# Up product of a decoder trunk: two of seven block products without the two leading columns, and the streamed operands at residues 0 and 128 modulo 256 bytes

## The chip, the cores and the metric

The kernel runs on one core of a Trainium2 chip. The metric is the device time of one execution in microseconds. Times are medians of a few executions; the profile is one further execution, whose span and whose own time are both given below. Engines are named as the profile does: PE is TensorE (matmuls; PEld its weight loads), DVE is VectorE, ACT is ScalarE, POOL is GpSimd, SP is SyncE, which issues the DMAs.

## The reference, cut to what matters

One layer of a decoder trunk over 1024 tokens and 16 meta tokens, model width 1024, float32. Two token mixers (a convolution module and a windowed attention) are merged and added to the residual, then comes the feed-forward part, which this change concerns:

```python
h = layer_norm(DEEPNORM_ALPHA * h + mixed @ w_out, ln1_g, ln1_b)
up = causal_dwconv(h @ ffn_w_up, ffn_dw, ffn_dw_b)      # 3 taps, 2 x 2816 channels
u, g = jnp.split(up, 2, axis=-1)
f = (jax.nn.gelu(g, approximate=False) * u) @ ffn_w_down
return layer_norm(DEEPNORM_ALPHA * h + f, ln2_g, ln2_b)
```

The convolution is causal with three taps, so the up product of a token needs that of the two tokens before it. Where the 1024 tokens are cut into two halves of 512, the second half needs the last two columns of the first half's product.

## The kernel before, in words

**Precision.** A float32 product is made of three matmuls in the type float32r: each operand is split into a high and a low part (the high part is a copy by ACT, the low part a subtraction by DVE), and high x high, high x low and low x high are added up in PSUM.

**Stages.** The big input product and the mixers run to about 415 us of the profile, the projections (tile ps_p) to about 512, the rows of the output product with their LayerNorm and their turning into columns (ps_w, ps_h) to about 609, the up product to 1049.6, the down product (ps_x, ps_z at L1619) to the end.

**The up product (L1462 to L1546).** The 1024 input channels are cut into two halves, the 1024 tokens into two halves h = 0, 1, and the output channels into gate and value. This two by two by two product is done by Strassen's scheme in Winograd's form with seven block products instead of eight: B11, B21, BT2, BT4, BT1, BT3, B22, in this order. The names are those of the streamed operand: B11 and the like are blocks of the input h, BT1 to BT4 sums and differences of them, formed once (form_t2, form_t3, form_t4) and split once into high and low parts (bsplit, split_of, L1174 to L1208). The stationary operands, sums of weight blocks, are formed and split anew in each block of output channels (up_weights L1321, wsplit L1299) and looked ahead by nine sets (w_ahead(9) in prod); they go around a ring of ten slots.

The outer loop goes over c = 0 to 21, each with 128 gate channels and 128 value channels. I call one turn of it a block. In a block, prod(q, bank, first) (L1475) does one of the seven products: for each sub, for each of four chunks k of 128 input channels, three matmuls. That is twelve matmuls, called a run here. There are two subs, because each half's 512 tokens with the two leading columns for the convolution make HW = 514 columns: SUB = [(0, 258), (258, 514)]. Sub 0 has 258 columns, the two leading ones among them, and sub 1 has 256. So a block has 7 x 2 runs of 12 matmuls, and the stage 22 x 168 = 3696. In block 0 all of sub 1 comes first and sub 0 after it, since the last input rows come late; in all others sub 0 and sub 1 alternate in each product.

The leading columns of the first half are the last two meta tokens, those of the second half the last two tokens of the first. Both are written to a tile edge while rows are turned into columns (turn, L1282 for the meta rows, and L1290, with eight small ACT activations, for the second half) and copied into place by edges (two copies, L1367).

**Where the operands lie.** B_AT (L1144) gives for each sub and product the tile and the offset (in float32 elements) of the high part; the low part follows, and the chunks k follow each other by 258 or by 256 elements. In the built program the tiles that hold them (OA, OC, RHC, RHO, RX) begin at 192 modulo 256 bytes, and so does each stationary operand. With the offset's 4 bytes per element that gives the residue of a streamed operand modulo 256 bytes. Before, sub 0 begins at 192 (B11, B21, BT2, BT4, B22), 0 (BT1) and 64 (BT3), and moves on by 8 bytes with each k; sub 1 lies at 0 throughout.

**What follows each product.** PSUM has four accumulators (X, Z, V4, Y, tiles px, pz, pw, py), used at columns 254 + a to 254 + b, so that sub 0 ends at a bank's end and sub 1 starts at the next bank. ACT copies (L1498) and DVE adds and subtractions (L1494, rank RK_CHAIN) make four results of 514 columns: c11 (gate, first half) and c21 (value, first half) in the tile FA, one after the other, c12 and c22 (gate and value, second half) in RT, a part of the tile OB, one after the other. Then come the three taps (conv_ffn: ACT L1413, DVE L1414 and L1415), the gelu on ACT, the product of gate and value on DVE, and the store (f_out). Interleaved, sums_load and sums_form prepare sums for the down product (DVE, L1446 and the following lines). The order of each engine is decided by a scheduler from ranks and data; PE's order in this stage is held as written by explicit links (last_mm).

Of the kernel before, what the change touches and what calls it, by code (L numbers as in the profile page):

```python
# [29 lines left out]
P = 128  # L30
# [71 lines left out]
def tile_hybrid_layer(  # L102
# [919 lines left out]
    rx_p = ctx.enter_context(tc.tile_pool(name="rx", bufs=1, side="right", reuse_waits="tile"))  # L1022
    RX = rx_p.tile([P, 2064], R, name="RX")
    rx_p.tile([P, 48], F, name="pad_x")
    wo_stack = ExitStack()
# [36 lines left out]

    pair = const.tile([P, KC, 4], R, name="pair")
    g_next = [0]

# [73 lines left out]
    def quadrant(sub, kk, h):  # L1139
# [3 lines left out]

    B_AT = [[(RHC, 6208), (RHO, 4096), (OA, 0), (OA, 2064), (OA, 4128), (OA, 6208), (RX, 0)],  # L1144
            [(OC, 16), (OC, 2064), (OC, 4112), (OC, 6160), (RHC, 2064), (RHC, 16), (RHC, 4112)]]
    B11, B21, BT2, BT1, BT3, BT4, B22 = range(7)

    def bsum(sub, q, hl):
        n = SUB[sub][1] - SUB[sub][0]
        t, o = B_AT[sub][q]  # L1150
        return t[:, o + hl * 4 * n:o + (hl + 1) * 4 * n]

    def bmat(sub, q, hl, k):
        n = SUB[sub][1] - SUB[sub][0]
        return bsum(sub, q, hl)[:, k * n:(k + 1) * n]
# [18 lines left out]
    def bsplit(sub, q, src, cs=slice(None)):  # L1174
        with rank(RK_SUMS):
            hi, lo = (wide(bsum(sub, q, hl))[:, :, cs] for hl in range(2))
            src = wide(src)[:, :, cs]
            ins = nc.scalar.copy(hi, src)
            if (sub, q) in ((0, BT2), (0, BT4), (0, BT1), (0, BT3)):
                if high:  # L1180
                    after(ins, high[-1])
                high.append(ins)
            line(nc.vector.tensor_tensor(lo, src, f32(hi), OP.subtract))
# [30 lines left out]
    WO_ORDER = (4, 5, 0, 1, 2, 3, 6, 7)  # L1214
    edge = const.tile([P, 2, KC, 2], F, name="edge")
    r_next = [1]
# [53 lines left out]
    def turn(i, r, n, ins, banks=None, behind=None, upper=False):  # L1270
        with rank(RK_TURN):
            for j, k0 in enumerate((4, 0) if upper else (0, 4)):
# [6 lines left out]
                for k in range(k0, k0 + 4):  # L1279
                    src = ps[:, (k - k0) * P:(k - k0) * P + n]  # L1280
                    if n < P:
                        dst = edge[:, 0, k]  # L1282
                    else:
# [4 lines left out]
                    nc.scalar.activation(dst, src, AF.Identity, bias=b1col(k), scale=g1col(k))  # L1288
                    if i == 3:
                        nc.scalar.activation(edge[:, 1, k], src[:, P - 2:P], AF.Identity, bias=b1col(k), scale=g1col(k))  # L1290
        return behind[-1] if behind else None
# [72 lines left out]
    def edges():  # L1364
        for h in range(2):
            with rank(RK_TURN):
                nc.vector.tensor_copy(FA[:, h * 2064:h * 2064 + 2064].rearrange("p (k n) -> p k n", n=258)[:, :, 0:2],  # L1367
                                      edge[:, h])

# [94 lines left out]
    for c in range(FC):  # L1464
        V4, X, Z, Y = (pup.tile([P, 1024], F, name=n, tag=n) for n in ("pw", "px", "pz", "py"))
        passes = ((1,), (0,)) if c == 0 else ((0, 1),)
        for subs in passes:
            last = subs == passes[-1]
            w_next = iter(range(7))
            a, b = SUB[subs[0]][0], SUB[subs[-1]][1]  # L1470

            def at(t):
                return t[:, 254 + a:254 + b]

            def prod(q, bank, first):  # L1475
# [5 lines left out]
                for sub in subs:  # L1481
                    o = bank[:, 254 + SUB[sub][0]:254 + SUB[sub][1]]
                    for k in range(4):
# [37 lines left out]
            prod(BT1, Y, True)  # L1521
            copy(c22[:, a:b], at(Y))
            prod(BT3, X, False)
            copy(u13[:, a:b], at(X))
            ins = tt(c22[:, a:b], c22[:, a:b], u13[:, a:b], OP.add)
            if last and c not in (0, FH + 1):
                sums_form(c - 1 if c <= FH else c - 2, ins)
            tt(c21[:, a:b], u13[:, a:b], at(V4), OP.subtract)
            prod(B22, Y, False)
            tt(c12[:, a:b], at(Y), u2[:, a:b], OP.add)  # L1530
            if last:
# [242 lines left out]
```

## Time and profile before

| what | us |
| --- | --- |
| median of 3 runs | 1269.1 (1268.91 to 1269.28) |
| profiled execution, its own time | 1269.45 |
| its span in the profile | 1267.2 |
| up product, PE | 609 to 1049.6 |
| PE busy in the 437.00 us from 609 to 1046 | 435.79 |
| DVE busy there | 396.05 |
| ACT busy there | 231.92 |

How to read it: the span is the profile's time from the first to the last instruction, and 2.25 us of the execution lie around it. The busy time of an engine says how much of a stretch it had work, not that it sets the time; which engine sets it is read from the chain of work that ended last and from idle times. Matmuls overlap on PE, so the duration of one is longer than its share of the time; the distance between two starts is that share. The mean granted clock of PE is 0.998.

### The profile page before, as it was taken

What the parts mean: (1) busy time and instruction counts of PE and PEld (TensorE: products, weight loads), DVE (VectorE), ACT (ScalarE), POOL (GpSimd) and SP (SyncE); (2) the same over time, 40 slices, a digit from 0 to 9 for tenths busy, and PEclk for the clock granted to TensorE, in tenths of its full rate; (3) what the DMA queues carried; (4) which work ended last, traced back from release to release, by engine and by line L of the source; (5) the groups of instructions that cost most, each with busy time, mean ns of one, the idle gap of its engine ahead of it and who ended that gap; (6) DMA issues with size and microseconds to landing.
All of it is one profiled execution on the core that took longest, in us unless ns stands there. A gap on an engine that the chain in (4) does not pass through costs nothing.

```text
span 1267.2 us, 21681 instructions
## 1 busy us (share of the span) xinstructions
PE 1255.8 (99%) x8546; PEld 1188.9 (94%) x8546; DVE 1084.1 (86%) x1837; ACT 588.5 (46%) x1065; POOL 54.0 (4%) x28
## 2 busy tenths in 40 slices
PE   9999999999999999999999999999999999999997
PEld 8999999999999999788899999999999998888886
DVE  7899989999989577548999999988889887896697
ACT  7522254545573233335655555454455544445330
POOL 0000000010122232000000000000000000000000
PEclk9999999999999999999999999999999999999999
DMA  7294633332146564222145546453454567989622
GB/s 277 72 302 112 188 94 96 105 96 85 68 138 184 163 164 124 84 85 82 67 157 195 194 171 214 161 208 126 158 203 172 192 211 287 389 309 349 241 92 84
DMA packets 96152, 212.10 MB, mean 167 GB/s; under 512 B 10787, under 2 KB 35939, under 8 KB 95922
## 3 DMA queue, kind: packets, MB, share of 16 engines
q1 hardware_dynamic: 84282, 199.64, 47.0%
q10 hardware_dynamic: 11768, 11.08, 2.7%
q8 instruction: 67, 1.10, 0.4%
q14 instruction: 35, 0.29, 0.1%
HBM read 150.29 MB, written 62.70 MB: 168 GB/s over the span
## 4 chain that ended last, share of the span: by engine, by line
PE 96%; ACT 1%; DVE 1%; DMA 1%; issue 0%; SPq 0%; ACTq 0%; DVEq 0%
PE px L1486 15%; PE py L1486 10%; PE ps_x L1619 9%; PE ps_z L305 8%; PE ps_z L301 8%; PE ps_z L306 8%; PE ps_z L1619 7%; PE pz L1486 5%; PE pw L1486 5%; PE ps_p L306 2%; PE ps_p L301 2%; PE ps_p L305 2%; PE ps_w L306 2%; PE ps_w L301 2%; PE ps_w L305 2%; PE ps_z L517 2%
## 5 line engine op out<-in xcount | busy, mean ns | idle before, releaser
L669 DVE SCALAR_TENSOR_TENSOR FA<-cin,cols,FA 128x1026 f32<-128x1026 f32 x120 | 155.1, 1304 | 0.2
L301 PE MATMUL ps_z<-RHO,whi 128*128 128x384 f32 (+2 forms) x324 | 104.7, 323 | 0.2 <-ACT FA L676 0.2
L305 PE MATMUL ps_z<-RHC,whi 128*128 128x384 f32 (+2 forms) x324 | 104.5, 323 | 0.0
L305 PE MATMUL ps_z<-RHO,whi 128*128 128x384 f32 (+2 forms) x324 | 104.0, 321 | 0.0
L306 PE MATMUL ps_z<-RHC,wlo 128*128 128x384 f32 (+2 forms) x324 | 103.8, 320 | 0.0
L301 PE MATMUL ps_z<-RHC,whi 128*128 128x384 f32 (+2 forms) x324 | 103.7, 320 | 0.0
L306 PE MATMUL ps_z<-RHO,wlo 128*128 128x384 f32 (+2 forms) x324 | 103.4, 319 | 0.0
L1308 DVE TENSOR_TENSOR RHO<-wr,RHO 128x512 fp32r<-128x512 f32 x94 | 63.4, 683 | 9.2 <-ACT RHO L1307 9.2
L1307 ACT CAST RHO<-wr 128x512 fp32r<-128x512 f32 x94 | 56.7, 619 | 21.7 <-DVE wr L1325 11.6
L273 ACT CAST whi<-wr 128x1024 fp32r<-128x1024 f32 x37 | 38.9, 1051 | 56.3 <-PE ps_z L305 36.9
L301 PEld LDWEIGHTS ps_z<-RHO,whi 128*128 128x128 f32 x324 | 60.9, 188 | 0.9 <-ACT FA L676 0.4
L305 PEld LDWEIGHTS ps_z<-RHC,whi 128*128 128x128 f32 x324 | 60.9, 188 | 0.4
L306 PEld LDWEIGHTS ps_z<-RHC,wlo 128*128 128x128 f32 x324 | 60.9, 188 | 0.2
L301 PEld LDWEIGHTS ps_z<-RHC,whi 128*128 128x128 f32 x324 | 60.9, 188 | 0.2
L306 PEld LDWEIGHTS ps_z<-RHO,wlo 128*128 128x128 f32 x324 | 61.0, 188 | 0.1
L305 PEld LDWEIGHTS ps_z<-RHO,whi 128*128 128x128 f32 x324 | 60.9, 188 | 0.1
L1325 DVE TENSOR_TENSOR wr<-wr 128x512 f32<-128x512 f32 x88 | 59.9, 681 | 0.2
L1498 ACT COPY FA<-px 128x514 f32<-128x514 f32 (+2 forms) x23 | 13.1, 572 | 80.7 <-PE px L1486 80.7
L276 POOL TENSOR_TENSOR wlo<-wr,whi 128x1024 fp32r<-128x1024 f32 x17 | 42.2, 2481 | 185.4 <-ACT whi L273 167.1
L676 ACT ACTIVATE FA<-ps_z,cols 128x386 f32<-128x386 f32 (+2 forms) x48 | 26.0, 542 | 46.6 <-PE ps_z L306 45.4
L1308 DVE TENSOR_TENSOR ws<-wr,ws 128x512 fp32r<-128x512 f32 x60 | 40.5, 684 | 5.3 <-ACT ws L1307 5.2
L1486 PE MATMUL px<-OA,RHO 128*128 128x258 f32 x324 | 43.3, 282 | 0.0
(466 smaller groups left out, 3577.4 us busy)
## 6 DMA issues: line engine op xcount, KB each, us to landing
wr<-in_w_up_dram SPq DMA_DIRECT2D x44, 512.0 KB, 4.1
wr<-in_w_z_dram SPq DMA_DIRECT2D x30, 512.0 KB, 3.7
fd<-FA SPq DMA_DIRECT2D x44, 256.0 KB, 2.4
OB<-in_w_down_dram SPq DMA_DIRECT2D x19, 512.0 KB, 6.2
qt<-qd SPq DMA_DIRECT2D x28, 256.0 KB, 3.8
td<-OB SPq DMA_DIRECT2D x12, 512.0 KB, 3.3
sums<-fd SPq DMA_DIRECT2D x12, 512.0 KB
sd<-sums SPq DMA_DIRECT2D x12, 512.0 KB, 2.7
```

The costliest lines, as they stand in the source:

```text
L273: ins = nc.scalar.copy(hi, raw)
L276: return (nc.vector if quick else nc.gpsimd).tensor_tensor(lo, raw, f32(hi), OP.subtract)
L301: ins = nc.tensor.matmul(ps, ah, bh, start=i == 0, stop=False)
L305: nc.tensor.matmul(ps, ah, bl, start=False, stop=False)
L306: last = nc.tensor.matmul(ps, al, bh, start=False, stop=i == n - 1)
L669: nc.vector.scalar_tensor_tensor(acc[c], cin[:, j:j + U], wc, acc[c], OP.mult, OP.add)
L676: nc.scalar.activation(t, ps, AF.Tanh, bias=bcol(14 + i), scale=0.5)
L1307: nc.scalar.copy(hi, src)
L1308: ins = nc.vector.tensor_tensor(lo, src, f32(hi), OP.subtract)
L1325: ins = nc.vector.tensor_tensor(*x)
L1486: ins = nc.tensor.matmul(o, x[:, ks], bmat(sub, q, hl, k), start=first and k + j == 0, stop=k == 3 and j == 2, skip_group_check=not first)
L1619: nc.tensor.matmul(banks[i], l[:, ts], r[:, ws], start=first and a and x + k == 0, stop=z and x == len(ops) - 1 and k == 2, skip_group_che ...
```

## The change

* The block products BT3 and B22 of sub 0 run over 256 columns, without the two leading ones (columns() gives their range). The leading columns of the second half's input are set to zero (a memset in place of the second copy in edges), so that these two products would have zeros there; the eight activations that wrote the second half of edge are gone, and edge is half as large.
* The second half's two leading columns of the result are no longer computed: after the last subtraction that c21 needs, one DVE copy for each block takes the last two columns of c11 and c21 to the first two of c12 and c22. The copy to c22 and the adds into c22 and c12 cover columns 2 to 514 instead of 0 to 514.
* B_AT has other offsets, and BT1 and B22 and others change places among the tiles. Of sub 0, the five products of 258 columns begin at residue 0 modulo 256 bytes and move on by 8 bytes with each k, the two of 256 columns lie at 128 throughout; sub 1 lies at 128 throughout.
* RX becomes 48 elements longer and takes the place of the tile pad_x, and a pad stands beside pair in place of the other half of edge; the addresses of the other tiles stay as they were, and the weights too.
* In the built program PE's order stays; DVE has 22 copies more, and in most blocks the add into c22, the subtraction into c21, the copy and the add into c12 follow each other directly.

```diff
--- before.py
+++ after.py
@@ -1020,8 +1020,7 @@
 
     tmp_stack.close()
     rx_p = ctx.enter_context(tc.tile_pool(name="rx", bufs=1, side="right", reuse_waits="tile"))
-    RX = rx_p.tile([P, 2064], R, name="RX")
-    rx_p.tile([P, 48], F, name="pad_x")
+    RX = rx_p.tile([P, 2112], R, name="RX")
     wo_stack = ExitStack()
     RW = wo_stack.enter_context(tc.tile_pool(name="rw", bufs=1, side="right", reuse_waits="tile")).tile(
         [P, 2048], R, name="RW")
@@ -1061,6 +1060,7 @@
         wo[k] = (hi, lo)
 
     pair = const.tile([P, KC, 4], R, name="pair")
+    const.tile([P, 16], F, name="pad_e")
     g_next = [0]
 
     GS = [(FA, i * 516) for i in range(4)]
@@ -1141,17 +1141,24 @@
         return FA[:, h1_at(sub, i):h1_at(sub, i + 4)]
 
 
-    B_AT = [[(RHC, 6208), (RHO, 4096), (OA, 0), (OA, 2064), (OA, 4128), (OA, 6208), (RX, 0)],
-            [(OC, 16), (OC, 2064), (OC, 4112), (OC, 6160), (RHC, 2064), (RHC, 16), (RHC, 4112)]]
+    B_AT = [[(RHC, 6224), (RHO, 4112), (OA, 16), (RX, 16), (OA, 2096), (OA, 6224), (OA, 4144)],
+            [(OC, 48), (OC, 2096), (OC, 4144), (OC, 6192), (RHC, 2096), (RHC, 48), (RHC, 4144)]]
     B11, B21, BT2, BT1, BT3, BT4, B22 = range(7)
 
+    def columns(sub, q):
+
+        a, b = SUB[sub]
+        return (2 if q in (BT3, B22) else a) if sub == 0 else a, b
+
     def bsum(sub, q, hl):
-        n = SUB[sub][1] - SUB[sub][0]
+        a, b = columns(sub, q)
+        n = b - a
         t, o = B_AT[sub][q]
         return t[:, o + hl * 4 * n:o + (hl + 1) * 4 * n]
 
     def bmat(sub, q, hl, k):
-        n = SUB[sub][1] - SUB[sub][0]
+        a, b = columns(sub, q)
+        n = b - a
         return bsum(sub, q, hl)[:, k * n:(k + 1) * n]
 
     lined, high = [], []
@@ -1173,8 +1180,11 @@
 
     def bsplit(sub, q, src, cs=slice(None)):
         with rank(RK_SUMS):
-            hi, lo = (wide(bsum(sub, q, hl))[:, :, cs] for hl in range(2))
-            src = wide(src)[:, :, cs]
+            a = columns(sub, q)[0] - SUB[sub][0]
+            x, y, _ = cs.indices(SUB[sub][1] - SUB[sub][0])
+            x = max(x, a)
+            hi, lo = (wide(bsum(sub, q, hl))[:, :, x - a:y - a] for hl in range(2))
+            src = wide(src)[:, :, x:y]
             ins = nc.scalar.copy(hi, src)
             if (sub, q) in ((0, BT2), (0, BT4), (0, BT1), (0, BT3)):
                 if high:
@@ -1212,7 +1222,7 @@
 
 
     WO_ORDER = (4, 5, 0, 1, 2, 3, 6, 7)
-    edge = const.tile([P, 2, KC, 2], F, name="edge")
+    edge = const.tile([P, KC, 2], F, name="edge")
     r_next = [1]
 
     def out_rows(i, between=(), work=()):
@@ -1279,15 +1289,13 @@
                 for k in range(k0, k0 + 4):
                     src = ps[:, (k - k0) * P:(k - k0) * P + n]
                     if n < P:
-                        dst = edge[:, 0, k]
+                        dst = edge[:, k]
                     else:
                         h, jj = divmod(i, 4)
                         sub = 0 if jj < 2 else 1
                         a = 2 + jj * P - SUB[sub][0]
                         dst = h1F(sub, h, k)[:, a:a + P]
                     nc.scalar.activation(dst, src, AF.Identity, bias=b1col(k), scale=g1col(k))
-                    if i == 3:
-                        nc.scalar.activation(edge[:, 1, k], src[:, P - 2:P], AF.Identity, bias=b1col(k), scale=g1col(k))
         return behind[-1] if behind else None
 
 
@@ -1362,10 +1370,11 @@
             w_ahead(n)
 
     def edges():
-        for h in range(2):
-            with rank(RK_TURN):
-                nc.vector.tensor_copy(FA[:, h * 2064:h * 2064 + 2064].rearrange("p (k n) -> p k n", n=258)[:, :, 0:2],
-                                      edge[:, h])
+        with rank(RK_TURN):
+            first, second = (FA[:, h * 2064:h * 2064 + 2064].rearrange("p (k n) -> p k n", n=258)[:, :, 0:2]
+                             for h in range(2))
+            nc.vector.tensor_copy(first, edge)
+            nc.vector.memset(second, 0.0)
 
     ahead = []
     work = {0: [(split_of, 1, B11), (split_of, 1, B21), (split_of, 1, B22)],
@@ -1468,8 +1477,9 @@
             last = subs == passes[-1]
             w_next = iter(range(7))
             a, b = SUB[subs[0]][0], SUB[subs[-1]][1]
-
-            def at(t):
+            i = max(a, 2)
+
+            def at(t, a=a):
                 return t[:, 254 + a:254 + b]
 
             def prod(q, bank, first):
@@ -1479,7 +1489,8 @@
                 else:
                     ah, al = w_ready[next(w_next)]
                 for sub in subs:
-                    o = bank[:, 254 + SUB[sub][0]:254 + SUB[sub][1]]
+                    x, y = columns(sub, q)
+                    o = bank[:, 254 + x:254 + y]
                     for k in range(4):
                         ks = slice(k * P, (k + 1) * P)
                         for j, (x, hl) in enumerate(((ah, 0), (ah, 1), (al, 0))):
@@ -1519,15 +1530,20 @@
                 g0 = gelu(conv_ffn(c11, FC + c))
             prod(BT4, V4, True)
             prod(BT1, Y, True)
-            copy(c22[:, a:b], at(Y))
+            copy(c22[:, i:b], at(Y, i))
             prod(BT3, X, False)
             copy(u13[:, a:b], at(X))
-            ins = tt(c22[:, a:b], c22[:, a:b], u13[:, a:b], OP.add)
+            ins = tt(c22[:, i:b], c22[:, i:b], u13[:, i:b], OP.add)
             if last and c not in (0, FH + 1):
                 sums_form(c - 1 if c <= FH else c - 2, ins)
             tt(c21[:, a:b], u13[:, a:b], at(V4), OP.subtract)
+            if last:
+                with rank(RK_CHAIN):
+                    ends, starts = (t.rearrange("p (i n) -> p i n", i=2)[:, :, x:x + 2]
+                                    for t, x in ((FA[:, 4128:4128 + 2 * HW], HW - 2), (RT[:, 0:2 * HW], 0)))
+                    nc.vector.tensor_copy(starts, ends)
             prod(B22, Y, False)
-            tt(c12[:, a:b], at(Y), u2[:, a:b], OP.add)
+            tt(c12[:, i:b], at(Y, i), u2[:, i:b], OP.add)
             if last:
                 f1 = conv_ffn(c22, c)
                 f_out(c, 0, g0, conv_ffn(c21, c))
```

## The prediction

> **What bounds the kernel now.** I read the page's busy times first, then the chain of work that ended last, then the stages one by one, and at last the timeline of TensorE over a single block of the up product.
>
> ```profile
> span 1267.2 us, 21681 instructions
> PE 1255.8 (99%) x8546; PEld 1188.9 (94%) x8546; DVE 1084.1 (86%) x1837; ACT 588.5 (46%) x1065; POOL 54.0 (4%) x28
> PE 96%; ACT 1%; DVE 1%; DMA 1%; issue 0%; SPq 0%; ACTq 0%; DVEq 0%
> PE px L1486 15%; PE py L1486 10%; PE ps_x L1619 9%; PE ps_z L305 8%; PE ps_z L301 8%; PE ps_z L306 8%; PE ps_z L1619 7%; PE pz L1486 5%; PE pw L1486 5%; PE ps_p L306 2%; PE ps_p L301 2%; PE ps_p L305 2%; PE ps_w L306 2%; PE ps_w L301 2%; PE ps_w L305 2%; PE ps_z L517 2%
> ```
>
> TensorE is 96% of the chain, and the four L1486 entries (15 + 10 + 5 + 5%) are the up product. Now three stretches (columns: length, then busy time of PE, PEld, DVE, ACT, POOL, the granted clock, the DMA share, GB/s): the stage of the output rows, a piece of the up product, and the down product.
>
> ```profile
> 505.00:609.00 104.00, 104.00 (x505) 83.74 (x504) 65.17 (x116) 44.11 (x107) 2.39 (x1) 1.00 0.23 82
> 740.00:840.00 100.00, 100.00 (x849) 100.00 (x848) 92.18 (x149) 51.11 (x86) 0.00 (x0) 1.00 0.52 187
> 1038.00:1267.00 229.00, 221.22 (x1024) 184.82 (x1022) 179.91 (x257) 87.05 (x100) 0.00 (x0) 0.99 0.69 249
> ```
>
> In the up product TensorE never idles and the clock is at its full value, so the stage lasts as long as its matmuls follow one another. A matmul's own duration is no measure of that, because matmuls overlap; the distance from one start to the next is. The timeline of one block (one value of c, fourteen runs of twelve matmuls, each product first sub 0 with 258 columns and then sub 1 with 256) gives it; columns are start, length, engine, line, output and inputs, shape, count.
>
> ```profile
> 831.20 1.60 PE L1486 MATMUL px<-RHC,ws 128*128 128x258 f32 x12
> 832.63 1.57 PE L1486 MATMUL px<-OC,ws 128*128 128x256 f32 x12
> 834.05 1.58 PE L1486 MATMUL pz<-RHO 128*128 128x258 f32 x12
> 835.47 1.57 PE L1486 MATMUL pz<-OC,RHO 128*128 128x256 f32 x12
> 836.88 1.58 PE L1486 MATMUL px<-OA,RHO 128*128 128x258 f32 x12
> 838.30 1.57 PE L1486 MATMUL px<-OC,RHO 128*128 128x256 f32 x12
> 839.71 1.58 PE L1486 MATMUL pw<-OA,RHO 128*128 128x258 f32 x12
> 841.13 1.57 PE L1486 MATMUL pw<-RHC,RHO 128*128 128x256 f32 x12
> 842.55 1.59 PE L1486 MATMUL py<-OA,RHO 128*128 128x258 f32 x12
> 843.98 1.57 PE L1486 MATMUL py<-OC,RHO 128*128 128x256 f32 x12
> 845.39 1.62 PE L1486 MATMUL px<-OA,RHO 128*128 128x258 f32 x12
> 846.85 1.58 PE L1486 MATMUL px<-RHC,RHO 128*128 128x256 f32 x12
> 848.26 1.59 PE L1486 MATMUL py<-RX,RHO 128*128 128x258 f32 x12
> 849.69 1.52 PE L1486 MATMUL py<-RHC,RHO 128*128 128x256 f32 x12
> 851.05 0.52 PE L1486 MATMUL px<-RHC,ws 128*128 128x258 f32 x3
> ```
>
> Subtract each start from the next. The block takes 851.05 - 831.20 = 19.85 us. Sub 0 takes 1.43 (B11), 1.42, 1.42, 1.42, 1.43 (BT1), 1.46 (BT3), 1.43 (B22); sub 1 takes 1.42, 1.41, 1.41, 1.42, 1.41, 1.41 and, for B22, 1.36. That last number matters most. The same shape, 256 columns, runs at 1.36 or at 1.41 to 1.42 for twelve, 113 or 118 ns each, and BT3 of sub 0 stands out upwards with 122 ns. So something other than the width sets part of the distance. That 1.36 is no accident of one block: the groups over all blocks give B22's matmuls (py from RHC) a shorter mean too (column: busy, mean ns).
>
> ```profile
> L1486 PE MATMUL px<-OC,RHO 128*128 128x256 f32 x260 | 34.2, 279 | 0.0
> L1486 PE MATMUL py<-RHC,RHO 128*128 128x256 f32 x120 | 15.2, 276 | 0.0
> ```
>
> The chain has the same period in every block, and hands the end on to the down product without a gap:
>
> ```profile
> 1004.38 2.87 PE px L1486 x24
> 1024.23 2.87 PE px L1486 x24
> 1044.09 2.87 PE px L1486 x24
> 1049.75 10.45 PE ps_z L1619 x46
> ```
>
> 1024.23 - 1004.38 = 19.85 again. What a block gains or loses passes to the end 22 times over, as the down product is on TensorE too (221.22 of 229.00 us busy).
>
> **The change part by part.**
>
> *Two columns fewer.* In BT3 and B22, 24 matmuls of a block go from 258 to 256 columns, 528 in all. What that is worth depends on what sets the distance. The rows bound it by their own spread: BT3 of sub 0 goes from 1.46, and B22 of sub 0 from 1.43, to what 256 columns cost, 1.36 to 1.42, so 0.05 to 0.17 us a block together. The Trainium skill ("TensorE: Matmul & The Clock Gate", section "Back-to-back issue gap") gives N/2.4 + 2.5 ns for a lone warm matmul; an estimate from it is 0.83 ns for two columns, 0.02 us a block, 0.4 us in all. The trace disagrees with the rule in that one width has two distances.
>
> *Placement.* All tiles that hold the operands begin at 192 modulo 256 bytes in the built program, both before and after. From the offsets in B_AT, the 256-wide operands of sub 1 go from residue 0 to 128; the new 256-wide ones of sub 0 also come to 128 (BT3 from 64, B22 from 192); the five that stay 258 wide start at 0 (before: 192, BT1 at 0), and move by 8 bytes from one k to the next. The weights stay at 192. No run of the trace has twelve matmuls in sequence at 128, so I bound the cost of a run from both sides: 1.36 (B22 of sub 1, the fastest) and 1.46 (BT3 of sub 0, the slowest, from 64). The nearest rows are in the projection, whose 256-wide matmuls draw two of every six operands from 128 and the others from 0, 64 and 192. The first and the last of 49 starts:
>
> ```profile
> 442.67 0.28 PE L301 MATMUL ps_p<-OA,whi 128*128 128x256 f32 x1
> 448.32 0.28 PE L301 MATMUL ps_p<-OA,whi 128*128 128x256 f32 x1
> ```
>
> 5.65 us / 48 = 117.7 ns, or 1.41 for twelve. So a third of operands at 128 cost a mixture nothing, and gave it nothing visible; it speaks against 1.46. I take 1.39, midway between the two values that the 256-wide runs of the block itself show (1.36 and 1.41 to 1.42), and keep both ends. The choice between them is the weak point of this forecast. For the five 258-wide runs at 0 I take 1.43, that of BT1, the one that stands there now; their rows now lie at 1.42 to 1.43, so the ends are close.
>
> The sum for a block: now nine runs (seven of sub 1, BT3 and B22 of sub 0) take 1.42 + 1.41 + 1.41 + 1.42 + 1.41 + 1.41 + 1.36 + 1.46 + 1.43 = 12.73, and five take 1.43 + 3 x 1.42 + 1.43 = 7.12. After: 9 x 1.39 = 12.51 and 5 x 1.43 = 7.15. That is 19.66 against 19.85, -0.19 a block, -4.2 us in 22 blocks.
>
> The skill has a rule against any such gain: by the same page, section "Step-by-step: what each phase is for", streamed operand and weights have two independent read ports, and it names no cost of an address. By it placement changes nothing. The 1.36 and 1.41 above speak for some dependence, but don't show that the address is what decides; this is the third rival.
>
> *One copy a block on VectorE.* It moves 4 elements in each partition, the last two columns of c11 and c21 to the first two of c12 and c22. The nearest row is the copy of the edges, 16 elements:
>
> ```profile
> L1367 DVE COPY FA<-edge x2: 161/168/176, 552.7 to 592.7; 128x16 f32<-128x16 f32 x2
> ```
>
> At most 0.17 us. VectorE is busy 92.18 of 100 us, 18.3 of a block's 19.85; with the copy 18.5 of 19.66. TensorE still covers that, if only 1.2 us are left. If the cover were gone, every tenth would count 22 times (2.2 us).
>
> *Order on VectorE.* By the built program, in most blocks the add into c22, the subtraction into c21, the copy and the add into c12 now come one after the other. Now three others stand ahead of the add into c12:
>
> ```profile
> 829.29 0.70 DVE L1494 TENSOR_TENSOR OB<-OB 128x514 f32<-128x514 f32 x1 [1.14 <-ACT OB L1498]
> 829.90 0.68 DVE L1494 TENSOR_TENSOR FA<-OB,pw 128x514 f32<-128x514 f32 x1
> 830.50 0.69 DVE L1446 TENSOR_TENSOR sums<-sums 128x512 f32<-128x512 f32 x1
> 831.10 0.75 DVE L1414 SCALAR_TENSOR_TENSOR FA<-OB,cols,FA 128x512 f32<-128x512 f32 x1
> 831.76 0.69 DVE L1447 TENSOR_TENSOR sums<-sums 128x512 f32<-128x512 f32 x1
> 832.37 0.69 DVE L1494 TENSOR_TENSOR OB<-py,FA 128x514 f32<-128x514 f32 x1
> ```
>
> The add needs B22, whose run ends where the next begins, at 831.20 plus a drain. Without the three it would stand ready at 829.90 + 0.68 + 0.17 = 830.75 and hold the sums and the convolutions behind it for 0.5 to 0.8 us. I cost this at nothing: a VectorE that is late finds TensorE's results ready and waits less, so only its busy 18.5 us bind.
>
> *Eight activations less, one memset for a copy, adds 512 for 514 wide.* They lie at 532 to 537 us and in the shadow of a TensorE that is busy for all 104.00 us from 505 to 609; ScalarE then waits on VectorE:
>
> ```profile
> L1290 ACT ACTIVATE edge<-ps_h,cols x8: 342/389/438, 532.7 to 536.8; 128x2 f32<-128x2 f32 x8
> 540.50 0.29 ACT L248 ACTIVATE sd<-mv,eps 128x1 f32<-128x1 f32 x1 [3.20 <-DVE mv L243]
> ```
>
> The 8 x 0.39 = 3.1 us make that wait longer. Nothing for the end. No DMA is added or moved in the built order, and TensorE's order is the same.
>
> The profiled execution took 1269.45 us, 2.25 more than its span and 0.35 more than the median of 1269.1. 1269.45 - 4.2 - 0.35 = 1264.9; I say **1265**.
>
> **The rivals.** The total depends on x, the run of twelve at 128: 9x + 7.15 equals 19.85 at x = 1.41. 0.2% (2.5 us, about what a measurement of this kernel can tell from no change) is 0.115 a block, so it is faster below 1.40 and slower above 1.42.
>
> 1. *All nine runs at 1.36.* For: one run of 256 columns has that in every block. Against: it has it alone, at residue 0, with six others there at 1.41. 9 x 1.36 + 7.15 = 19.39, -0.46 a block, -10.1 us: 1259.
>
> 2. *Placement does nothing.* For: the projection's mixture and six of seven runs are at 1.41; so 9 x 1.413 + 7.15 = 19.87, +0.02 a block, +0.4 us: 1269.5. It is also the case in which the change doesn't do what it says.
>
> 3. *Residue 128 is a bad place.* The other side, at the reads of the 108 matmuls of a block at 128: if these cost what BT3's run costs from 64, 9 x 1.46 + 7.15 = 20.29, +0.44, +9.7 us: 1279. It decides from x = 1.42. For: a step of some bytes already costs 0.05 us a run in this very kernel. Against: the projection's 117.7 ns.
>
> 4. *VectorE's new wait binds.* If the waits did not shrink, its block would be 18.5 + 1.14 (for the copy, row above) + 0.8 = 20.4 us, more than TensorE's; the look-ahead of nine weight sets would run dry after some blocks and the gain would be lost, with up to 0.55 x 22 = 12 us on top. I expect a part of that at most: about 1272.
>
> **How the numbers follow.** Forecast 0.33, rival 1 0.15, rival 2 0.29, rival 3 0.14, rival 4 0.09. Faster 0.48, same 0.29, slower 0.23. The range runs from 1258.5 (rival 1) to 1273 (rival 4's part); it leaves out rival 3 and the larger part of rival 4, some 0.2.
>
> **What would show it.** In the timeline of one block: nine runs of 1.39 and five of 1.43, a period of 19.66 in the chain, no idle time of TensorE between 640 and 1040. Runs of 1.36 are rival 1; 1.41, rival 2; over 1.42, rival 3. For rival 4 TensorE would show idle time ahead of L1486 released by ScalarE or VectorE. The forecast is wrong from the root if the distance of 256 columns hangs on what precedes a run, not on where its operand lies: then runs at one residue would again differ among themselves.

## The result and the profile after

The changed kernel takes **1259.53 us** (median of 6 runs, 1259.31 to 1259.90) against 1269.10 of before: a ratio of 0.9925 (95% interval 0.9915 to 0.9934), 9.6 us less. It is inside the predicted range, 5.5 us below the forecast of 1265, and half a microsecond from the first rival's 1259. The profiled execution took 1259.33 us, 2.23 more than its span.

The page after, the span and the busy times:

```profile
span 1257.1 us, 21713 instructions
PE 1246.0 (99%) x8546; PEld 1179.2 (94%) x8546; DVE 1086.6 (86%) x1859; ACT 587.4 (47%) x1057; POOL 54.1 (4%) x28
```

Of the 10.1 us of the span, 9.8 are gone from the busy time of PE (1255.8 to 1246.0), with as many matmuls as before. A stretch of the up product after (columns as before: length, busy times, clock, DMA share, GB/s) has PE busy all the time and the clock at 1.00, as before; so the matmuls follow one another faster, and nothing else has become the bound:

```profile
640.00:1038.00 398.00, 398.00 (x3448) 398.00 (x3447) 371.30 (x607) 212.31 (x348) 0.00 (x0) 1.00 0.53 187
```

The timeline of PE over one block after, and the first row of the next. In order: B11, B21, BT2, BT4, BT1, BT3, B22, each with sub 0 first.

```profile
826.02 1.59 PE L1497 MATMUL px<-RHC,ws 128*128 128x258 f32 x12
827.46 1.52 PE L1497 MATMUL px<-OC,ws 128*128 128x256 f32 x12
828.81 1.60 PE L1497 MATMUL pz<-RHO 128*128 128x258 f32 x12
830.25 1.52 PE L1497 MATMUL pz<-OC,RHO 128*128 128x256 f32 x12
831.61 1.59 PE L1497 MATMUL px<-OA,RHO 128*128 128x258 f32 x12
833.04 1.52 PE L1497 MATMUL px<-OC,RHO 128*128 128x256 f32 x12
834.40 1.59 PE L1497 MATMUL pw<-OA,RHO 128*128 128x258 f32 x12
835.84 1.52 PE L1497 MATMUL pw<-RHC,RHO 128*128 128x256 f32 x12
837.19 1.60 PE L1497 MATMUL py<-RX,RHO 128*128 128x258 f32 x12
838.63 1.52 PE L1497 MATMUL py<-OC,RHO 128*128 128x256 f32 x12
839.99 1.52 PE L1497 MATMUL px<-OA,RHO 128*128 128x256 f32 x12
841.35 1.52 PE L1497 MATMUL px<-RHC,RHO 128*128 128x256 f32 x12
842.71 1.52 PE L1497 MATMUL py<-OA,RHO 128*128 128x256 f32 x12
844.07 1.52 PE L1497 MATMUL py<-RHC,RHO 128*128 128x256 f32 x12
845.43 0.77 PE L1497 MATMUL px<-RHC,ws 128*128 128x258 f32 x5
```

Subtract each start from the next again. The nine runs of 256 columns take 1.35 to 1.36 each, 12.22 us together (12.73 before), the five of 258 columns 1.43 to 1.44, 7.19 together (7.12 before). The block takes 845.43 - 826.02 = 19.41 instead of 19.85; -0.44 in 22 blocks is -9.7 us, the whole result. A 256-wide run has two paces in the two kernels, 1.36 and 1.41 to 1.42 (113 and 118 ns a matmul). I call them the short and the long pace. Before, one of seven runs of sub 1 had the short one; now all nine have it. The question for the experiments is what decides the pace.

The chain has the same distance, 1039.66 - 1020.25 = 19.41, from the last block's first piece to the down product:

```profile
1020.25 2.79 PE px L1497 x24
1039.66 20.41 PE ps_z L1635 x90
```

VectorE at the end of one block, behind the subtraction into c21:

```profile
825.39 0.69 DVE L1455 TENSOR_TENSOR sums<-sums 128x512 f32<-128x512 f32 x1
825.99 0.17 DVE L1544 COPY OB<-FA 128x4 f32<-128x4 f32 x1
826.11 0.69 DVE L1456 TENSOR_TENSOR sums<-sums 128x512 f32<-128x512 f32 x1
826.72 0.68 DVE L1505 TENSOR_TENSOR OB<-py,FA 128x512 f32<-128x512 f32 x1
```

The copy takes 0.17 us and has no idle time ahead of it. The add into c12 does not stand directly behind it: of the two sums shown, L1455 lies ahead of the copy and L1456 behind it, and the add starts at 826.72. B22's run ended where the next began, at 826.02.

### The profile page after: what moved, and what is told of

It reads as the page before. It is cut to its first block, busy times and chain, and to the rows that moved or that the text cites. A ratio compares the mean times of both kernels' runs of the same rounds, so it can differ in the third digit from the quotient of the medians.

```text
span 1257.1 us, 21713 instructions
## 1 busy us (share of the span) xinstructions
PE 1246.0 (99%) x8546; PEld 1179.2 (94%) x8546; DVE 1086.6 (86%) x1859; ACT 587.4 (47%) x1057; POOL 54.1 (4%) x28
## 4 chain that ended last, share of the span: by engine, by line
PE 96%; ACT 1%; DVE 1%; DMA 0%; issue 0%; ACTq 0%; DVEq 0%; SPq 0%
PE px L1497 14%; PE py L1497 9%; PE ps_x L1635 9%; PE ps_z L305 8%; PE ps_z L301 8%; PE ps_z L306 8%; PE ps_z L1635 7%; PE pz L1497 5%; PE pw L1497 5%; PE ps_p L306 2%; PE ps_p L301 2%; PE ps_p L305 2%; PE ps_w L306 2%; PE ps_w L301 2%; PE ps_w L305 2%; PE ps_z L517 2%
## 5 line engine op out<-in xcount | busy, mean ns | idle before, releaser
L1422 ACT ACTIVATE FA<-OB,cols 128x512 f32<-128x512 f32 x44 | 35.9, 816 | 14.0 <-DVE OB L1505 14.0
```

Source lines behind the costliest of these rows:

```text
L1422: nc.scalar.activation(t, cc[:, 2:HW], AF.Identity, bias=ffw(3, o), scale=ffw(2, o))
```

## The experiments

Each kernel was timed against the kernel before on the same chip. Those of experiments 6 and 8 were executed once, so their times are rough and their timelines are what counts. "Runs" are again the twelve matmuls of one product and sub, a run's time is the distance from its start to the next run's, and a "place" is the residue modulo 256 bytes at which the streamed operand begins.

**1. The columns alone.** The changed kernel with the old B_AT.

```diff
-    B_AT = [[(RHC, 6224), (RHO, 4112), (OA, 16), (RX, 16), (OA, 2096), (OA, 6224), (OA, 4144)],
-            [(OC, 48), (OC, 2096), (OC, 4144), (OC, 6192), (RHC, 2096), (RHC, 48), (RHC, 4144)]]
+    B_AT = [[(RHC, 6208), (RHO, 4096), (OA, 0), (OA, 2064), (OA, 4128), (OA, 6208), (RX, 0)],
+            [(OC, 16), (OC, 2064), (OC, 4112), (OC, 6160), (RHC, 2064), (RHC, 16), (RHC, 4112)]]
```

> The columns alone: the changed kernel with the operands at the places of before (sub 1 at 0; sub 0 at 192, BT1 at 0, BT3 at 64). Address theory (a run of twelve with 256 columns takes 1.36 us at residue 128, 1.41 at 0): sub 1 stays at 1.41, BT3 and B22 of sub 0 fall from 1.46 and 1.43 to about 1.41, the block from 19.85 to about 19.78, the time to about 1267.5. Columns theory (the two columns make the whole gain): block 19.41, time 1259.5.

Measured: 1268.71 us, ratio 0.9998 (0.9989 to 1.0008): no gain. A few runs of its timeline, B22 of sub 0 and of sub 1, then B11:

```profile
827.87 1.60 PE L1497 MATMUL py<-RX,ws 128*128 128x256 f32 x12
829.30 1.58 PE L1497 MATMUL py<-RHC,ws 128*128 128x256 f32 x12
830.72 1.60 PE L1497 MATMUL px<-RHC,ws 128*128 128x258 f32 x12
832.16 1.52 PE L1497 MATMUL px<-OC,ws 128*128 128x256 f32 x12
833.52 1.60 PE L1497 MATMUL pz<-RHO 128*128 128x258 f32 x12
```

With 256 columns, from 192, B22 of sub 0 still takes 829.30 - 827.87 = 1.43. And the one run of sub 1 with the short pace is another: it is no longer B22 (1.42) but B11, at 832.16 (1.36), though both lie at 0 in both kernels. So the pace of a run at 0 hangs on what happened ahead of it. The columns theory (1259.5) falls. The address theory (1267.5) comes nearer to the total, but it is wrong on both details.

**2. Sub 1 alone to 128, in the kernel before.**

```diff
-            [(OC, 16), (OC, 2064), (OC, 4112), (OC, 6160), (RHC, 2064), (RHC, 16), (RHC, 4112)]]
+            [(OC, 48), (OC, 2096), (OC, 4144), (OC, 6192), (RHC, 2096), (RHC, 48), (RHC, 4144)]]
```

> The kernel before with only sub 1 moved from residue 0 to 128; all widths and sub 0 as before. Address theory: all seven runs of sub 1 at 1.36 whatever stands ahead of them, block 19.85 - 6 x 0.053 = 19.53, time about 1262. Entry theory (a run of 256 columns keeps the pace at which the run ahead of it hands over, its own place doesn't matter): sub 0 is untouched, so 1.41 as before and 1269. Columns theory: 1269.

Measured: 1268.41 us, ratio 0.9995 (0.9986 to 1.0004). The total is what the entry and the columns theory said (1269), but not for their reasons: sub 1 does take the short pace or nearly so (1.36 to 1.38), which the entry theory denies, and the columns theory fell in experiment 1. The gain of the address theory is missing all the same. B21 of sub 0 and sub 1, and the run behind them:

```profile
832.94 1.63 PE L1486 MATMUL pz<-RHO 128*128 128x258 f32 x12
834.41 1.53 PE L1486 MATMUL pz<-OC,RHO 128*128 128x256 f32 x12
835.78 1.63 PE L1486 MATMUL px<-OA,RHO 128*128 128x258 f32 x12
```

Sub 1 takes 1.37 (1.41 before), but the 258-wide run from 192 ahead of it now takes 1.47 (1.42 before). What a run gains here, its neighbour loses, and it is so in four of the seven pairs. The address theory misses this because it counts each run by itself. Two pairs gain at no cost to the neighbour: BT3, and above all BT1, whose sub 0 starts at 0 as in the changed kernel and takes 842.90 - 841.46 = 1.44, sub 1 then 844.26 - 842.90 = 1.36. The pair of B22 only loses, since its sub 1 had the short pace already.

**3. Sub 1 alone back to 0, in the changed kernel.**

```diff
-            [(OC, 48), (OC, 2096), (OC, 4144), (OC, 6192), (RHC, 2096), (RHC, 48), (RHC, 4144)]]
+            [(OC, 16), (OC, 2064), (OC, 4112), (OC, 6160), (RHC, 2064), (RHC, 16), (RHC, 4112)]]
```

> The changed kernel with only sub 1 moved back to residue 0. Address theory: sub 1 at 1.41 again, with B22 of sub 1 perhaps at 1.36 as before; block 19.41 + 6 x 0.053 = 19.73, time about 1266.5; BT3 and B22 of sub 0, at 128, stay at 1.36. Entry theory and columns theory: nothing changes, 1259.5.

Measured: 1267.61 us, ratio 0.9986 (0.9977 to 0.9996). BT3 of sub 0 (at 128) and of sub 1 (at 0), then B22 of sub 0:

```profile
824.52 1.53 PE L1497 MATMUL px<-OA,ws 128*128 128x256 f32 x12
825.89 1.57 PE L1497 MATMUL px<-RHC,ws 128*128 128x256 f32 x12
827.30 1.53 PE L1497 MATMUL py<-OA,ws 128*128 128x256 f32 x12
```

128 takes 1.37 and 0 takes 1.41. This time the address theory is right on these runs (not on B22 of sub 1, which has 1.41 too), and entry and columns theory fall.

**4. The weights by 128 bytes.** Six of the ten weight slots, those in RHO, move from 192 to 64; B21 of sub 0 makes room and keeps its place 0.

```diff
-    B_AT = [[(RHC, 6224), (RHO, 4112), (OA, 16), (RX, 16), (OA, 2096), (OA, 6224), (OA, 4144)],
+    B_AT = [[(RHC, 6224), (RHO, 4176), (OA, 16), (RX, 16), (OA, 2096), (OA, 6224), (OA, 4144)],
...
-    RING = [RHO[:, i * 1024:(i + 1) * 1024] for i in range(4)]
+    RING = [RHO[:, 32 + i * 1024:32 + (i + 1) * 1024] for i in range(4)]
     RING += [None] * 4
-    RING += [RHO[:, 6208 + i * 1024:6208 + (i + 1) * 1024] for i in range(2)]
+    RING += [RHO[:, 6240 + i * 1024:6240 + (i + 1) * 1024] for i in range(2)]
```

> The changed kernel with six of the ten weight slots (those in RHO) moved by 128 bytes, from residue 192 to 64, and B21 of sub 0 moved to make room, at residue 0 as it was. Address theory in its plain form: nothing changes, 1259.5. Distance theory (the place of the streamed operand counts from that of the weights): the 256-wide runs whose weights are in RHO go from 1.36 to about 1.41 and those with weights in ws stay at 1.36; six tenths of nine runs by 0.05 are 0.28 us a block, time about 1265.5.

Measured: 1270.48 us, ratio 1.0010 (1.0001 to 1.0020). The time misleads here. By the program, two of the moved slots reach 32 elements into the next group of rows that the output product reads, and what this kernel returns is no longer the layer's output. PE waits 7.2 us ahead of the up product, and its granted clock is 0.98 (505 to 609 us) and 0.94 (609 to 640 us) instead of 1.00. That the overlap causes the wait is argued, not shown.

```profile
PE ps_h L1285 <- DVE OB L1275: 7.2, 2, 3.6
```

```profile
818.88 1.53 PE L1497 MATMUL px<-OC,RHO 128*128 128x256 f32 x12
820.24 1.60 PE L1497 MATMUL pz<-RHO 128*128 128x258 f32 x12
...
830.08 1.52 PE L1497 MATMUL py<-OC,ws 128*128 128x256 f32 x12
831.43 1.52 PE L1497 MATMUL px<-OA,ws 128*128 128x256 f32 x12
```

(the wait first, with total, times and longest; then the timeline). In the up product itself, a 256-wide run with its weights in RHO takes 820.24 - 818.88 = 1.36, one with weights in ws 831.43 - 830.08 = 1.35; no 256-wide run from 820 to 850 us takes more than 1.37. So 128 bytes in the place of the weights do next to nothing, where the distance theory asked for 1.41; in this form it falls.

**5. The places alone.** The kernel before, with all seven products of sub 0 at 258 columns; for want of room BT3 lies at 128 and B22 at 64. RX is 48 elements longer, as in the changed kernel.

```diff
-    B_AT = [[(RHC, 6208), (RHO, 4096), (OA, 0), (OA, 2064), (OA, 4128), (OA, 6208), (RX, 0)],
-            [(OC, 16), (OC, 2064), (OC, 4112), (OC, 6160), (RHC, 2064), (RHC, 16), (RHC, 4112)]]
+    B_AT = [[(RHC, 6224), (RHO, 4112), (OA, 16), (RX, 16), (OA, 6256), (OA, 2128), (OA, 4192)],
+            [(OC, 48), (OC, 2096), (OC, 4144), (OC, 6192), (RHC, 2096), (RHC, 48), (RHC, 4144)]]
```

> The places alone: the kernel before, all of sub 0 at 258 columns and no copy, with sub 1 at 128, five products of sub 0 at 0 as in the changed kernel, and, for want of room, BT3 at 128 and B22 at 64. Settling theory (a 256-wide run at 128 settles at 1.36 in a few matmuls, a 258-wide one takes 1.434 from 0 and up to 1.47 elsewhere): 7 x 1.36 + 5 x 1.434 + 2 x 1.45 = 19.59 a block against 19.85 of before and 19.41 of the changed kernel, time about 1263.4. Place theory of the prediction (places give all but 0.07 us a block): about 19.48, 1261. If the gain needs both parts: 19.85, 1269.

Measured: 1264.57 us against 1269.65, ratio 0.9958 (0.9944 to 0.9973): 5.1 us. The settling theory, at 1263.4, comes nearest; its miss is in one pair, BT3:

```profile
823.09 1.60 PE L1485 MATMUL px<-OA,ws 128*128 128x258 f32 x12
824.52 1.58 PE L1485 MATMUL px<-RHC,ws 128*128 128x256 f32 x12
825.94 1.62 PE L1485 MATMUL py<-OA,ws 128*128 128x258 f32 x12
```

At 128 behind a 258-wide run that starts at 128 too, sub 1 of BT3 has the long pace (825.94 - 824.52 = 1.42). So 128 isn't short by itself.

**6. Maps, two kernels executed once.** The five 258-wide runs, then the seven of sub 1, at other places.

```diff
-    B_AT = [[(RHC, 6224), (RHO, 4112), (OA, 16), (RX, 16), (OA, 2096), (OA, 6224), (OA, 4144)],
+    B_AT = [[(RHC, 6200), (RHO, 4136), (OA, 24), (RX, 32), (OA, 2096), (OA, 6256), (OA, 4144)],
```

> The changed kernel with its five 258-wide products at 160 (B11), 96 (B21), 32 (BT2), 128 (BT4) and 64 (BT1) in place of 0. If 0 is a good place for 258 columns by itself: these runs take 1.45 to 1.47, as at 192 and 64 in the run with sub 1 at 128, and the block is 19.41 + 5 x 0.025 = 19.5 or more. If only the width counts: 1.434 in each, 19.41.

```diff
-            [(OC, 48), (OC, 2096), (OC, 4144), (OC, 6192), (RHC, 2096), (RHC, 48), (RHC, 4144)]]
+            [(OC, 32), (OC, 2088), (OC, 4152), (OC, 6208), (RHC, 2072), (RHC, 8), (RHC, 4144)]]
```

> The changed kernel with sub 1 at 64 (B11), 96 (B21), 160 (BT2), 224 (BT4), 192 (BT1), 32 (BT3) and 128 (B22). If 128 alone is good for 256 columns, the six others take 1.39 to 1.42 and the block 19.6 to 19.75; if 0 alone is bad, all take 1.36 and the block stays at 19.41.

Measured: the first, 1262.37 us; 258 columns take 1.43 to 1.46 from all five places, so none is better than 0 (1.43), and sub 1 has the short pace (1.36 to 1.37) behind all but the run that starts at 128 (BT4), where it has the long one (1.41 to 1.42). The second, 1267.24 us; the six places 32, 64, 96, 160, 192 and 224 give 1.40 to 1.43 for 256 columns of sub 1, and 128 gives 1.36. BT3 and B22 of sub 0 stay at 128 but now follow a run at 192 or 32, and they take 1.38: their first four matmuls are slower (114 to 122 ns), the others have 113. So a run can also come to the short pace on its way, and values between the two paces do occur.

**7. All at 128, and the mirror image.** First the five 258-wide products move from 0 to 128 too; then the places are exchanged: these at 128, all nine 256-wide ones at 0.

```diff
-    B_AT = [[(RHC, 6224), (RHO, 4112), (OA, 16), (RX, 16), (OA, 2096), (OA, 6224), (OA, 4144)],
+    B_AT = [[(RHC, 6256), (RHO, 4144), (OA, 48), (RX, 48), (OA, 2160), (OA, 6256), (OA, 4208)],
```

> The changed kernel with its five 258-wide products moved from 0 to 128, so that all fourteen runs lie at 128. Hand-over theory (a 256-wide run has two paces, 1.36 and 1.41, and the place of the run ahead of it relative to its own decides which one it is in; from the same place it is 1.41, as BT3 and BT4 showed in two runs): nine runs at 1.41 and five at 1.433, block 19.9, time about 1270. Address theory (128 is good, whatever stands ahead): block 19.41, 1259.5.

```diff
-    B_AT = [[(RHC, 6224), (RHO, 4112), (OA, 16), (RX, 16), (OA, 2096), (OA, 6224), (OA, 4144)],
-            [(OC, 48), (OC, 2096), (OC, 4144), (OC, 6192), (RHC, 2096), (RHC, 48), (RHC, 4144)]]
+    B_AT = [[(RHC, 6256), (RHO, 4144), (OA, 48), (RX, 48), (OA, 2128), (OA, 6256), (OA, 4176)],
+            [(OC, 16), (OC, 2064), (OC, 4112), (OC, 6160), (RHC, 2064), (RHC, 16), (RHC, 4112)]]
```

> The changed kernel with the two places exchanged: the five 258-wide products at 128, the nine 256-wide runs at 0. Hand-over theory (only the place relative to the run ahead counts): 1.36 in all nine, block 19.41, time 1259.5. Address theory (128 is better than 0 for 256 columns): 1.41 in all nine, block 19.88, time about 1270.

Measured: all at 128, 1270.35 us, ratio 1.0011 (1.0002 to 1.0021); the mirror, 1271.84 us, 1.0020 (1.0010 to 1.0029). BT3 of sub 0 and the start of sub 1 behind it, of the first kernel, then of the second:

```profile
825.40 1.58 PE L1497 MATMUL px<-OA,ws 128*128 128x256 f32 x12
826.82 1.58 PE L1497 MATMUL px<-RHC,ws 128*128 128x256 f32 x12
```

```profile
826.49 1.57 PE L1497 MATMUL px<-OA,ws 128*128 128x256 f32 x12
827.90 1.57 PE L1497 MATMUL px<-RHC,ws 128*128 128x256 f32 x12
```

Both have the long pace in all nine runs, 1.41 to 1.42. The very place that gives 1.36 in the changed kernel gives 1.41 here, run after run: the pure address theory falls. The mirror, at the same relative places, has the long pace as well: the hand-over theory in its relative form falls too. What remains is both together, the place and the sequence. In the steady blocks of all kernels so far, a 256-wide run at 128 goes to the short pace behind a run at another place (1.36 to 1.38), keeps the pace of a 256-wide run at 128 ahead of it, and has the long one behind 258 columns at 128. So the short pace need not be handed over: in experiment 3, B22 of sub 0 takes 1.37 right behind a run of 1.41 at 0. (At 0 the short pace showed in one run a block, before and in experiment 1.)

**8. Widths, two kernels executed once.** Some runs take other widths at the same places, by a moving operand that is cut off or read on into the next chunk. Both kernels leave out columns that the layer needs; only their pace is of use.

```diff
-                    x, y = columns(sub, q)
-                    o = bank[:, 254 + x:254 + y]
+                    a, b = columns(sub, q)
+                    n = {(1, BT2): 242, (1, BT3): 248, (1, B22): 240}.get((sub, q), b - a)
+                    o = bank[:, 254 + a:254 + a + n]
+                    if (sub, q) == (0, B21):
+                        n = 272
+                        o = bank[:, 240:512]
...
-                            ins = nc.tensor.matmul(o, x[:, ks], bmat(sub, q, hl, k), start=first and k + j == 0,
+                            t, f = B_AT[sub][q]
+                            f += (hl * 4 + k) * (b - a)
+                            ins = nc.tensor.matmul(o, x[:, ks], t[:, f:f + n], start=first and k + j == 0,
```

> The changed kernel with other widths, at the places it has: B21 of sub 0 over 272 columns in place of 258 (the 14 more are never read), and of sub 1 BT2 over 242, BT3 over 248 and B22 over 240 columns in place of 256, which leaves out the last columns of these products. Step theory (a matmul lasts a whole number of steps of 6.67 ns, of which 16 columns fill one): 272 columns cost what 258 cost, 1.434 to 1.44 for twelve; 242 and 248 cost what 256 cost, 1.36; 240 cost a step less, 1.28. Rate theory (every column costs 0.417 ns): 272 take 1.434 + 0.07 = 1.50, 248 take 1.32, 242 take 1.29, 240 take 1.28.

```diff
...
-                    o = bank[:, 254 + x:254 + y]
+                    a, b = columns(sub, q)
+                    n = {(0, BT2): 256, (1, B21): 258, (1, BT2): 260, (1, BT4): 264, (1, BT3): 254}.get((sub, q), b - a)
+                    o = bank[:, 254 + a:254 + a + n]
...
```

> The changed kernel with other widths at the places it has: of sub 1, B21 over 258, BT2 over 260, BT4 over 264 and BT3 over 254 columns, all from the same place 128 for each k (those beyond 256 are never read; BT3's last two are left out), and of sub 0 BT2 over 256 columns with its place moving on by 8 bytes as for 258 (two columns left out). Walk theory (what costs in the 258-wide runs is that the place moves on by 8 bytes): 258, 260 and 264 columns from one place take 1.37 to 1.40, and 256 moving columns 1.43. Width theory (what costs is a width over 256): 258 to 264 from one place take 1.43 to 1.47, and 256 moving columns 1.36 to 1.41. 254 take 1.36 by both, as 248 did.

Measured: 1264.88 and 1270.4 us. From the first, BT3 of sub 1 (248 columns), B22 of sub 0 (256) and of sub 1 (240), both runs of the next block's B11, B21 of sub 0 (272) and the start of the run behind it:

```profile
824.54 1.52 PE L1503 MATMUL px<-RHC,ws 128*128 128x248 f32 x12
825.90 1.57 PE L1503 MATMUL py<-OA,ws 128*128 128x256 f32 x12
827.31 1.51 PE L1503 MATMUL py<-RHC,ws 128*128 128x240 f32 x12
828.65 1.60 PE L1503 MATMUL px<-RHC,ws 128*128 128x258 f32 x12
830.09 1.57 PE L1503 MATMUL px<-OC,ws 128*128 128x256 f32 x12
831.50 1.68 PE L1503 MATMUL pz<-RHO 128*128 128x272 f32 x12
833.01 1.55 PE L1503 MATMUL pz<-OC,RHO 128*128 128x256 f32 x12
```

248 columns take 1.36, as 256 do, and 240 still 1.34; 272 take 1.51. The step theory fails at 240 and 272, the rate theory below 256. What the rows show is a floor of about 1.34 to 1.36 for twelve at 240 to 256 columns. They also break the description at the end of experiment 7. B11 of sub 1 (start 830.09) lies at 128 behind 258 columns from 0, exactly as in the changed kernel, where it takes 1.36; here it takes 1.41. What differs lies further back: the run before that has 240 columns instead of 256. So the pace hangs on more than the one run ahead, and behind narrower runs later ones were slower. From the second, B21 of sub 1 (258 columns, place fixed) and BT2 of sub 0 (256 columns, place moving on by 8 bytes):

```profile
835.47 1.61 PE L1500 MATMUL pz<-OC,RHO 128*128 128x258 f32 x12
836.91 1.59 PE L1500 MATMUL px<-OA,RHO 128*128 128x256 f32 x12
838.34 1.63 PE L1500 MATMUL px<-OC,RHO 128*128 128x260 f32 x12
```

1.44 and 1.43, so each theory is right in one half. A width over 256 alone, at a fixed place 128, costs what the 258-wide runs cost. The moving place alone is not settled by this: the 256 columns start at 0, where a fixed place has the long pace of 1.41 to 1.42 in most runs anyway. BT3 with 254 columns, behind runs of the long pace, took 1.42, so the pace counts there too.

**9. One product more.** BT1 of sub 0 also goes only into an accumulator (Y) whose leading columns nobody reads any longer, so it can do without them as well.

```diff
-        return (2 if q in (BT3, B22) else a) if sub == 0 else a, b
+        return (2 if q in (BT1, BT3, B22) else a) if sub == 0 else a, b
```

with BT1 at (RX, 48), that is at 128.

> A step further in the sense of the change: BT1 of sub 0 also without its two leading columns and at 128 (its sum goes to the accumulator Y alone, whose leading columns nobody reads since the copy). Hand-over theory, with BT4 of sub 1 at the fast pace ahead of it: BT1 falls from 1.434 to 1.36 and the five runs behind it keep 1.36; block 19.41 - 0.074 = 19.33, 1.6 us in 22 blocks, time about 1257.9. Rival: without the 258-wide run at 0 ahead of it, one of the runs from BT1 on falls to 1.41 and stays there to the block's end, as from BT1 on in the run with all at 128; then up to 6 x 0.053 = 0.3 us a block more, up to 1266. Rate theory of columns alone (two columns fewer in twelve matmuls): 0.01 us a block, 1259.3.

Measured: **1257.70 us**, ratio to before 0.9909 (0.9896 to 0.9923), the fastest of all. BT1 of sub 0 and of sub 1, and BT3 of sub 0:

```profile
836.37 1.52 PE L1497 MATMUL py<-RX,RHO 128*128 128x256 f32 x12
837.73 1.52 PE L1497 MATMUL py<-OC,RHO 128*128 128x256 f32 x12
839.09 1.18 PE L1497 MATMUL px<-OA,RHO 128*128 128x256 f32 x9
```

BT1 of sub 0 takes 1.36, and so does the run behind it: the short pace is handed on. The hand-over theory's 1257.9 is met, within 0.2 us. What the copy made possible is worth one more product than the change took.

## Why the prediction was right, and where it was off

**The bound** was right: PE sets the time, a block's difference passes to the end 22 times over (22 x 0.44 = 9.7 of 9.6 us), and nothing else came up.

**The run at 128** is the term that was mis-sized. I took 1.39, midway between 1.36 and 1.41 to 1.42; it measured 1.36 in all nine. Together they took 12.22 us instead of 12.51, which is 6.4 us in 22 blocks; the five 258-wide runs, at 7.19 instead of 7.15, take 0.9 back. That is the miss of 5.5. By the signs that the prediction itself named, runs of 1.36 are the first rival's, not the forecast's: the result lies in the range because the range was drawn down to that rival. A midpoint was the wrong sort of estimate. The rows showed two paces and nothing between them, so the sum was in the main a choice between the first and the second rival.

**What the sum left out** is the sequence. It priced each run by its own place and gave the neighbours no price. With all fourteen runs at 128 the same pricing gives about the same gain, and measured there is none (1270.35). That the five 258-wide runs came to 0, and so all nine others fell to the short pace, was nothing that the prediction had reckoned with; to that extent it was luck.

**The two columns.** I bounded them at 0.05 to 0.17 us a block by themselves. Alone they gave nothing that could be measured (1268.71 against 1269.04), the places alone 5.1 us (with two runs at other places, for want of room), both together 9.6. The parts are not a sum. Without the two columns a run can take the short pace, and at the right place, behind the right run, it does; at 258 columns none of the seven places tried (0, 32, 64, 96, 128, 160, 192) gave 1.36.

**The first rival** has the right time, and it was argued with the doubt that six runs at 0 took 1.41. That doubt was justified: at 128 too all runs can have the long pace (experiment 7). The warning at the end of the prediction, that the forecast is wrong from the root if the distance hangs on what precedes a run and not on its place, holds in part: experiments 1, 5, 7 and 8 show a change of pace where a run's own place stayed the same, experiments 2 and 3 one where the place moved.

**Placement does nothing** (second in the list of rivals, though an earlier sentence of the prediction calls it the third) is excluded by the places alone, 5.1 us in experiment 5, and by the sub 1 runs moved alone, 1.37 at 128 and 1.41 at 0. The rule behind it (the Trainium skill, "TensorE: Matmul & The Clock Gate", section "Step-by-step: what each phase is for"), which names two independent read ports and no cost of an address, doesn't cover what is measured here. The mixture in the projection, 117.7 ns, was no evidence on 128 either way: it never lets twelve matmuls follow at one place. **Residue 128 is bad** (third rival) asked for 1.46 and 1279; no 256-wide run at 128 took more than 1.42, and the kernel with all runs there took 1270.35, no more than the long pace that sub 1 had at 0 before.

**VectorE's wait** (fourth rival) didn't come. The copy measured 0.17 us as estimated, and VectorE was busy for 371.30 of 398.00 us, 93% where I had worked out 94%. But the order that I took from the built program, and that the description of the change repeats, isn't the one in the trace: in 21 of the 22 blocks other work lies between the copy and the add into c12, in 12 of them one sum and nothing else. In the whole stage the adds and subtractions of L1505 waited on PE once, 0.5 us for py. Costing it at nothing was right, but the reason I gave was not put to the test, since the order that it was meant for hardly occurred.

**Open.** What sets the two paces is not shown. The runs show that they are two, that a run keeps its pace as a rule once it has it, that the place of the streamed operand and the runs ahead of it decide together, further back than one run, and that 128 bytes in the place of the weights hardly matter. That the floor is the pace of the weight loads is only a guess from 240 columns being hardly faster than 256; no run changed the weight loads. Their busy time of all 398.00 us above does not show it: one load takes 188 ns and the next starts 113 to 118 ns later, so the loads overlap and the row would read the same at either pace. The Trainium skill ("TensorE: Matmul & The Clock Gate", section "Back-to-back issue gap") says that in a stream of weight load and matmul pairs both set the spacing. The floor would fit that in kind, but no run here shows it.

## What to carry to other kernels

Where matmuls follow one another without a gap, read the distance between starts run by run before pricing a change by columns: two paces for one shape mean that something besides the width is to be had, and that its price is mostly one pace or the other, not a mean. Test a placement with its neighbours: a run that was made shorter made the run beside it longer, and one place gave both paces in two sequences. Where an edit makes a value unread, ask which other work fed only that value; here it took one more product out of the wide shape.

## What the runs showed of the hardware

- A 256-column float32r matmul in this stream takes 113 or 118 ns from start to start (1.36 or 1.41 to 1.42 us for twelve), at the same clock of 1.00, and can keep its pace for a whole block (nine runs at 1.36 in one kernel, nine at 1.41 to 1.42 in another). A run that changes pace does so in its first matmuls: 1.38 for twelve, with four slower ones and then 113 ns.
- The place of the streamed operand modulo 256 bytes and the runs ahead decide which: 256 columns at 128 took 1.36 behind 258 columns from 0 and 1.41 to 1.42 behind 258 columns from 128. With 240 columns one run earlier, they took 1.41 behind 258 columns from 0 as well.
- Just under 256 columns there is next to nothing to gain: 248 columns take 1.36 us for twelve, 240 take 1.34.
- The step from 256 columns at the short pace to 258 costs 1.36 to 1.43 or 1.44, 6 ns a matmul, much more than two columns in proportion; from 258 to 272 it is 1.44 to 1.51.
